# Two blocks of the A/B projection accumulated in the opening of layer 0, and one modulation group moved from layer 0's gate/up to layer 1's

## The chip, the cores and the metric

The kernel runs as one program on one core of a Trainium2 chip. The metric is the device time of one execution in microseconds (us). A core has a matrix engine (TensorE, PE), a vector engine (VectorE, DVE), a scalar engine (ScalarE, ACT), a general engine (GpSimd, POOL), a queue engine (SyncE, SP) that here only starts transfers, and sixteen DMA engines. Each engine works off its own list of instructions in order and waits on semaphores of the others. PE writes its products to PSUM, from where other engines fetch them.

## The reference, cut to what matters

The program computes two layers of an encoder on a sequence of 1024 tokens of width 1024:

```python
mod = silu(c) @ w_mod[l] + b_mod[l]                    # 1024 -> 6 * 1024
sh_a, sc_a, gt_a, sh_f, sc_f, gt_f = split(mod, 6)     # six modulation groups
h = rms_norm(x, g_attn[l]) * (1 + sc_a) + sh_a
proj = h @ w_in[l]                                     # columns of heads A, B and C
ya = neighborhood_attention(...); yb = sliding_window_attention(...); yc = axial_attention(...)
x = x + gt_a * (concat(rms_norm(ya), rms_norm(yb), rms_norm(yc)) @ w_o[l])
h = rms_norm(x, g_ffn[l]) * (1 + sc_f) + sh_f
gate, up = split(h @ w_gu[l], 2)                       # 2 * 2816 columns
x = x + gt_f * ((silu(gate) * up) @ w_down[l])
```

and a last `rms_norm` behind the second layer. All is in 32-bit floating point.

## The kernel before

**Products.** Each 32-bit operand is split into a high and a low part (`hh`/`hl` for the normalised activations, `whi`/`wlo` for weights), and a product is three matmuls (`mm3`: high x high, high x low, low x high) that accumulate in one PSUM tile of 128x512. A split is two passes: ACT writes the high part (a cast or copy), DVE, or POOL at some places, subtracts it and writes the low one. The activations are kept transposed: `hh[:, k, c]` is block `k` of eight (128 of the 1024 features) for the tokens `c`. A half is 512 tokens (`H`); layer 0 builds `hh`/`hl` for half 0 in the opening, pair of blocks by pair, and those for half 1 at the end of the opening (`h_blocks`).

**The opening of layer 0** needs the first two modulation groups before it has any block of `h`. For each pair `p` of blocks, 0 to 3, two loads `gm` of `w_mod` are multiplied by the condition (`gemv_half`: DVE adds, then a few PE matmuls into `ps_mod`), turned (`gemv_turn`, `ps_m`), and finished into shift and scale, after which `h_blocks(0, ...)` makes the two blocks (`pair_done`). Beside that, `c_first(n)` accumulates the C columns of half 0, block by block, into the four tiles `pssC` that stay open from pair 0 to the C section: 12 matmuls per block. Their weights come by `wc_stage` (SP starts the load into one of a small set of stage buffers `wst`) and `w_split`. `x_turn(1, ...)` transposes the second half of `x` into eight PSUM tiles `ps_x`, which ACT copies to `xt`; `spread` and `turn_vecs` (`pst`) follow, then `c_norm_first` and the four `h_blocks(1, ...)`. The pool `psl` of the opening has eight PSUM tiles with one tag; a new tile waits until the readers of the tile before it in its place are done.

**The C section and V projection** (about 76 to 175 us). Step `t` projects 128 tokens of C (`c_proj`), normalises and rotates the tiles of the step before, and transposes those of the step before that. Beside them run the A/B blocks `oc` 0 and 1 (`NE = 2`), and their results are taken out of PSUM by `ab_split`, which ACT and DVE do, and stored to a table in memory (`qkd`). The list `abs_` holds blocks that are projected and not yet split. V follows.

**The A/B section** (about 175 to 247 us) goes over `oc` = 2 to 7 and the two halves: `ab_proj` (24 matmuls into `ps_ab`), the store of the block before, the load of the weights two blocks on, at some steps `mod_sum` (four `ps_mod` matmuls), `z_step` (parts of a bias table), a number of `mod_one` (one 512 KB load of `w_mod` and DVE passes), and `ab_split`. Attention, the output projection, gate/up and down follow.

**Gate/up** takes 22 quads of columns, each with seven products (Strassen's scheme, so that sums of blocks are multiplied). `mod_stream` is a generator of the modulation groups that are left: each `next` does one step of a group, a 256 KB load `wmt` and a DVE pass into `acc`, and at the end of a group two flushes (`mod_parts` writes `acch` and `accl` on DVE, `mod_flush` makes two matmuls into `ps_mod` and two DVE passes). One step is taken behind each product from quad 7 on.

**Order.** Within the stages that are pinned (`pin(..., True)`) each engine issues in the order in which the code is written; so the list of calls in the opening and the tuples of `mod_one` counts set the order of the work.

The profile gives line 49 for every instruction, since a helper issues them all; so names of tiles, not lines, tell them apart.

Of the kernel before, what the change touches and what calls it, by code (L numbers as in the profile page):

```python
# [19 lines left out]
P = 128  # L20
D = 1024
S = 1024
# [63 lines left out]
def trunk(ctx: ExitStack, tc, A, C, out):  # L86
# [583 lines left out]
    def wc_stage(kp):  # L670
        st = stage()
        for dst, v in w_in_src(0, C_COLS, kp)(parts(st, 2)):
            sp.dma_start(dst, v)
        wcs.append(st)

    def c_first(n):

        wh, wl = wC[n // 2]
        for t in range(T0):
# [3 lines left out]
                n == 0, n == KC - 1,  # L683
            )

    def spill(half, ns=range(KC)):
        c = slice(half * H, (half + 1) * H)
        for n in ns:
            sp.dma_start(xd[:, n, c], xt[:, n, c])
# [8 lines left out]

    NE = 2
    T0 = 4  # L700
    wC, wcs = [], []
    pin((pe, act, dve, sp), True)
    c8 = stp.tile([KC, P], F32, name="c8")
# [5 lines left out]
    gm_load(0)  # L709
    gm_load(1)  # L710
    wc_stage(0)
    gm_load(2)
    rxs = [stp2.tile([P, 4], F32, name="rx", tag="rx", bufs=2) for _ in range(2)]
    act.activation(c8, c8, AF.Silu)
# [28 lines left out]

    gemv_half(0)
    gm_load(3)
    wc_stage(1)
    keep_busy(4)
    gemv_half(1)
    gm_load(4)
    xns[1].append(x_load(1, 0))  # L750
    w_split()
    wc_stage(2)
    keep_busy(2)
    pair_done(0)
    pssC = [psl.tile([P, 512], F32, name="ps_c", tag="mm") for _ in range(T0)]
    gemv_half(2)
    gm_load(5)
    xns[1].append(x_load(1, 1))
    c_first(0)
    w_split()  # L760
    wc_stage(3)
    c_first(1)
    gemv_half(3)
    gm_load(6)
# [1 line left out]
    gemv_half(4)  # L766
    gm_load(7)
    xns[1].append(x_load(1, 3))
    pair_done(1)
    x_square(1, 0, xns[1][0], rxs[1])  # L770
    c_first(2)
    c_first(3)
    w_split()
# [5 lines left out]
    gemv_half(6)  # L779
    pair_done(2)  # L780
    x_square(1, 1, xns[1][1], rxs[1])
    c_first(4)
    c_first(5)
    w_split()
# [4 lines left out]
    for j in (2, 3):  # L789
        x_square(1, j, xns[1][j], rxs[1])  # L790
    x_rms(rxs[1])
    x_turn(1, xns[1], range(4), (act, act))
    c_first(6)
    x_turn(1, xns[1], range(4, KC), (act, act))
# [1 line left out]
    spill(1)  # L796
    rows = spread(rxs[1], 0, psl)
    turn_vecs(1, v1)
    gm = stp.tile([P, 2048], F32, name="gm", tag="gm", bufs=3)
    first_t1 = c_norm_first(pssC[0], gm[:, 0:512], gm[:, 512:1024], gm[:, 1024:1032])  # L800

# [17 lines left out]
    for l in range(2):  # L819
# [158 lines left out]
        psc, psv = dict(enumerate(pssC)), {}  # L978
        qts, qns = {0: first_t1}, {}
        w = split_tile(wab.pop(0), KC, (ct, "wx", 2), dve)  # L980
        abs_ = []
        wV, vst = [], []

        def v_stage(kp):
# [193 lines left out]
        for oc in range(NE, 8):  # L1178
            w = wab
            for half in range(2):  # L1180
                if half == 0 and oc < 7:
                    sc = -0.125 if oc < 3 else None
                    wab = split_tile(wst.pop(0), KC, eng=dve, scale=sc)
                if oc == 6 and half == 0:
                    close(ps_cm)
                    psS_cm, psS = open_pool("psS", bufs=2, space=PSUM)
                    ps_cm, psl = open_pool("ps2", bufs=4, space=PSUM)
                scored = early_scores() if oc == 7 else None
                ps = ab_proj(w, half)
                if store:  # L1190
                    store(act)
                if scored:
                    scored()
                if half == 0 and oc < 6:
                    wst.append(w_ab(l, oc + 2))
                i = 2 * (oc - NE) + half
                if i % 4 == 2:
                    mod_sum()
                z_step()
                for _ in range((2, 2, 2, 1, 2, 1, 2, 1, 2, 1, 0, 0)[i]):  # L1200
                    mod_one()
                store = ab_split(oc, half, ps, ab)
        store(act)
        pin((pe, act, dve, pool), False)
        close(ab_cm)
# [816 lines left out]
            shifted_sub(b21, b21, shift(2 * i + 1), t2)  # L2022
            h_split("t4", i, b21, dve)

        mods_due = mod_stream(psl, (ntp, "sq", 2, H), (1, 3))
        bs = []
        rows = None
        norm = rstd_rows(ssq, ntp, psl)
# [24 lines left out]
        for q in range(NF):  # L2053
# [9 lines left out]
            for i, p in enumerate(PRODUCTS[2 if q < EARLY else 0 :]):  # L2063
# [2 lines left out]
                    act.activation(e, quads[q]["11"], AF.Silu)  # L2066
                ahead.fill()
                g_step()
                if q >= EARLY:
                    next(mods_due, None)  # L2070
        for _ in mods_due:
            pass
# [329 lines left out]
```

## Time and profile before

| what | us |
|---|---|
| median of three runs | 2403.49 |
| lowest and highest | 2403.01, 2408.04 |
| the profiled execution | 2405.66 |
| its span on the core | 2403.9 |
| opening, to the first `c_proj` of half 1 | 76.0 |
| A/B section, end of the last `ps_ab` | about 247 |
| gate/up of layer 0 (576.8 to 1013.7) | 436.9 |
| gate/up of layer 1 (1749.7 to 2173.6) | 423.9 |

Of the span PE is busy 97%, DVE 73%, ACT 50% and POOL 31%; the mean granted clock of PE is 0.993 of full. A row of the timeline gives start and length in us, engine, operation, the tile written and the tiles read; the time in brackets is how long the engine stood before it, and behind the arrow is what ended the wait. Rows with a count (x4) are several instructions that follow on each other. Matmuls overlap, so the distance of their starts, not the length of one, is what a matmul costs.

### The profile page before, as it was taken

How to read it: one execution, taken by the hardware profiler on the slowest of the kernel's cores; microseconds unless marked ns; L12 is line 12 of the kernel's file. 1: busy time of each engine (PE TensorE's matmuls, PEld its weight loads, DVE VectorE, ACT ScalarE, POOL GpSimd, SP SyncE). 2: the span in 40 equal slices, each digit the busy share in tenths (PEclk: the TensorE clock that was granted, in tenths of full speed). 3: DMA queues.
4: the chain of work that ended last, by engine and by line, in shares of the span. 5: the costliest groups of instructions: out<-in, count | busy, mean ns of one | idle time of the engine just before them, and what ended most of it. 6: DMA issues, size and time to landing. Idle time of an engine off the chain costs nothing. (4 is left out here: it accounts for less than half of the span.)

```text
span 2403.9 us, 33342 instructions
## 1 busy us (share of the span) xinstructions
PE 2337.2 (97%) x11733; PEld 1954.9 (81%) x11733; DVE 1756.9 (73%) x2788; ACT 1192.2 (50%) x2250; POOL 744.0 (31%) x719
## 2 busy tenths in 40 slices
PE   8999999999999999999999999999999999999998
PEld 4788899888787887888887879988888888888886
DVE  5767898977858788587677679988797554547765
ACT  3422788944543333344543148897454334334443
POOL 1431345610244443300036114465004443430001
PEclk9999999999999999999999999999999999999999
DMA  8458316154345454586424761152534333329633
GB/s 265 138 183 278 94 62 156 45 201 129 109 137 171 155 186 152 174 265 197 155 88 123 246 215 28 44 145 74 199 103 145 114 101 106 122 88 298 213 125 110
DMA packets 305336, 356.95 MB, mean 148 GB/s; under 512 B 51964, under 2 KB 221788, under 8 KB 305168
## 3 DMA queue, kind: packets, MB, share of 16 engines
q1 hardware_dynamic: 283296, 342.07, 44.9%
q10 hardware_dynamic: 21504, 12.59, 2.0%
q8 instruction: 92, 1.51, 0.3%
q14 instruction: 76, 0.62, 0.1%
q0 software_dynamic: 368, 0.17, 0.0%
HBM read 269.79 MB, written 88.63 MB: 149 GB/s over the span
## 5 line engine op out<-in xcount | busy, mean ns | idle before, releaser
L49 PE MATMUL ps_d<-wpt 128*128 128x512 f32 x1848 | 423.8, 390 | 1.1 <-ACT wpt L49 0.7
L49 PEld LDWEIGHTS ps_d<-wpt 128*128 128x128 f32 x1848 | 345.7, 188 | 74.4 <-issue 3.0
L49 POOL TENSOR_SCALAR pr<-pr,rs 128x1024 f32<-128x1024 f32 (+2 forms) x248 | 193.0, 791 | 220.8 <-DVE rs L49 196.8
L49 POOL TENSOR_TENSOR sg<-sg,u 128x512 f32<-128x512 f32 x82 | 116.6, 1422 | 354.0 <-ACT sg L49 228.4
L49 PE MATMUL pv<-pt,vs 128*128 128x256 f32 x1088 | 175.8, 296 | 17.7 <-DVE y L49 13.4
L49 DVE TENSOR_TENSOR pt<-T,pt 128x512 fp32r<-128x512 f32 x272 | 176.9, 678 | 8.3 <-ACT pt L49 8.0
L49 ACT CAST wpt<-w 128x512 fp32r<-128x512 f32 x154 | 95.7, 621 | 174.6 <-PE ps_d L49 156.1
L49 ACT CAST pt<-T 128x512 fp32r<-128x512 f32 x272 | 151.8, 584 | 40.6 <-PE T L49 38.8
L49 ACT COPY u<-ps_w 128x512 f32<-128x512 f32 x128 | 75.1, 587 | 190.1 <-PE ps_w L49 190.1
L49 POOL TENSOR_TENSOR wpt<-ws,wpt 128x512 fp32r<-128x512 f32 x80 | 110.9, 1388 | 186.5 <-ACT wpt L49 140.3
L49 DVE TENSOR_TENSOR wpt<-w,wpt 128x512 fp32r<-128x512 f32 x154 | 108.9, 707 | 79.8 <-ACT wpt L49 77.7
L49 PEld LDWEIGHTS pv<-pt,vs 128*128 128x128 f32 x1088 | 141.7, 190 | 30.8 <-DVE y L49 26.0
L49 PE MATMUL T<-identr,pr 128*128 128x128 f32 x1176 | 161.6, 273 | 0.8 <-DVE edge L49 0.4
L49 PEld LDWEIGHTS T<-identr,pr 128*128 128x128 f32 x1176 | 137.9, 140 | 16.0 <-issue 1.3
L49 DVE SCALAR_TENSOR_TENSOR acc<-wmt,condT,acc 128x512 f32<-128x512 f32 (+1 forms) x98 | 113.9, 1172 | 44.6 <-DMA wmt<-in_w_mod_dram 44.2
L49 ACT CAST wpt<-ws 128x512 fp32r<-128x512 f32 x176 | 107.8, 622 | 60.0 <-issue 28.1
L49 DVE TENSOR_TENSOR wpt<-ws,wpt 128x512 fp32r<-128x512 f32 x96 | 82.9, 872 | 62.0 <-ACT wpt L49 61.9
L49 DVE TENSOR_TENSOR wpt<-graw,wpt 128x512 fp32r<-128x512 f32 x154 | 110.1, 715 | 17.4 <-ACT wpt L49 17.4
L49 ACT CAST wpt<-graw 128x512 fp32r<-128x512 f32 x154 | 95.0, 617 | 52.9 <-DMA graw<-gpd 48.8
L49 DVE TENSOR_REDUCE rs<-sC 128x1 f32<-128x1024 f32 x88 | 107.3, 1221 | 17.7 <-PE sC L49 12.3
L49 DVE TENSOR_TENSOR ws<-wr 128x512 f32<-128x512 f32 x88 | 78.9, 899 | 53.9 <-POOL wpt L49 50.8
L49 PE MATMUL sC<-qk 128*128 128x512 f32 x384 | 107.5, 403 | 5.8 <-ACT pr L49 5.6
(300 smaller groups left out, 5938.0 us busy)
## 6 DMA issues: line engine op xcount, KB each, us to landing
wr<-in_w_gu_dram SPq DMA_DIRECT2D x92, 512.0 KB, 4.1
gpd<-sg SPq DMA_DIRECT2D x154, 256.0 KB, 4.4
graw<-gpd SPq DMA_DIRECT2D x76, 512.0 KB, 3.5
w<-in_w_down_dram SPq DMA_DIRECT2D x110, 256.0 KB, 5.6
wmt<-in_w_mod_dram SPq DMA_DIRECT2D x48, 512.0 KB, 5.3
qk<-qkd SPq DMA_DIRECT2D x44, 512.0 KB, 7.1
wst<-in_w_o_dram SPq DMA_DIRECT2D x32, 512.0 KB, 4.1
wmt<-in_w_mod_dram SPq DMA_DIRECT2D x64, 256.0 KB, 3.6
```

Of the source, the lines that this page charges most:

```text
L49: ins = op(*args, **kwargs)
```

## The change

The four parts of the change are these.

1. *Opening.* `a_stage(u)` loads the weights of A/B block 2 + u, and `a_split(u)` splits them (one ACT and one DVE pass of 128x1024, with the factor -0.125) into blocks of `hh`/`hl` of the second half, 6 and 7 for u = 0, 4 and 5 for u = 1, which are not needed until `h_blocks(1, ...)`. `a_first(u, p)` does the six matmuls of half 0 for the pair `p` of blocks into `pssA[u]`. The last three `wc_stage` come one step later.
2. *C section.* `abs_` begins with these two finished blocks, so their `ab_split` stands ahead of the normalisation of C step 0 and their eight stores are started by SP.
3. *A/B section.* `oc` 2 and 3 leave out half 0; the counts of `mod_one` sum to 16 as before, in another order, and the first `mod_sum` comes one step later in layer 0.
4. *Gate/up.* The stream of layer 0 ends with group (1, 1) and not with (1, 2), so three groups are left there and not four; the A/B section of layer 1 takes (1, 2), (1, 3), (1, 4), and one group is left for layer 1's gate/up, (1, 5). No step is taken behind products 2 and 5 of a quad.

```diff
+    def a_stage(u):
+        ast.append(w_ab(0, EARLY_AB[u]))
+    def a_split(u):
+        st = parts(ast.pop(0), 2)
+        hi, lo = (t[:, 6 - 2 * u : 8 - 2 * u, H:S] for t in (hh, hl))
+        act.activation(hi, st, AF.Copy, scale=-0.125)
+        dve.scalar_tensor_tensor(
+            out=lo, in0=st, scalar=-0.125, in1=f32(hi), op0=ALU.mult, op1=ALU.subtract
+        )
+    def a_first(u, p):
+        for k in (2 * p, 2 * p + 1):
+            n, c = 6 - 2 * u + k // 4, slice(H + k % 4 * P, H + k % 4 * P + P)
+            mm3(
+                pssA[u], hh[:, n, c], hl[:, n, c], hh[:, k, 0:H], hl[:, k, 0:H],
+                k == 0, k == KC - 1,
+            )
...
+    EARLY_AB = (2, 3)
...
     wc_stage(0)
+    a_stage(0)
     gm_load(2)
...
     gemv_half(0)
     gm_load(3)
-    wc_stage(1)
     keep_busy(4)
     gemv_half(1)
     gm_load(4)
     xns[1].append(x_load(1, 0))
+    a_split(0)
     w_split()
-    wc_stage(2)
+    wc_stage(1)
     keep_busy(2)
     pair_done(0)
     pssC = [psl.tile([P, 512], F32, name="ps_c", tag="mm") for _ in range(T0)]
+    pssA = [psl.tile([P, 512], F32, name="ps_ab", tag="mm") for _ in range(2)]
     gemv_half(2)
     gm_load(5)
+    a_stage(1)
     xns[1].append(x_load(1, 1))
     c_first(0)
     w_split()
-    wc_stage(3)
+    wc_stage(2)
     c_first(1)
...
     xns[1].append(x_load(1, 3))
+    wc_stage(3)
     pair_done(1)
+    a_split(1)
     x_square(1, 0, xns[1][0], rxs[1])
+    a_first(0, 0)
     c_first(2)
     c_first(3)
...
     x_square(1, 1, xns[1][1], rxs[1])
+    a_first(1, 0)
+    a_first(0, 1)
     c_first(4)
     c_first(5)
...
     x_rms(rxs[1])
+    a_first(1, 1)
     x_turn(1, xns[1], range(4), (act, act))
     c_first(6)
     x_turn(1, xns[1], range(4, KC), (act, act))
...
     turn_vecs(1, v1)
+    for u in (1, 0):
+        for p in (2, 3):
+            a_first(u, p)
...
-        abs_ = []
+        abs_ = [] if l else [(oc, 0, ps) for oc, ps in zip(EARLY_AB, pssA)]
...
-                ps = ab_proj(w, half)
+                early = l == 0 and half == 0 and oc in EARLY_AB
+                ps = None if early else ab_proj(w, half)
...
-                if i % 4 == 2:
+                if i in ((2, 6, 10) if l else (3, 6, 10)):
                     mod_sum()
                 z_step()
-                for _ in range((2, 2, 2, 1, 2, 1, 2, 1, 2, 1, 0, 0)[i]):
+                for _ in range(
+                    (2, 2, 2, 1, 2, 1, 2, 1, 2, 1, 0, 0)[i]
+                    if l else (0, 2, 0, 3, 2, 2, 2, 2, 2, 1, 0, 0)[i]
+                ):
                     mod_one()
-                store = ab_split(oc, half, ps, ab)
+                store = None if early else ab_split(oc, half, ps, ab)
...
-        mods_due = mod_stream(psl, (ntp, "sq", 2, H), (1, 3))
+        mods_due = mod_stream(psl, (ntp, "sq", 2, H), (1 + l, 2 - 2 * l))
...
-                if q >= EARLY:
+                if q >= EARLY and i % 3 != 2:
                     next(mods_due, None)
```

The first place is on PE in the opening, the first four tiles of `x_turn(1, ...)` and the start of `c_first(6)` (`ps_x` is written by transposes of `xn`, the loaded rows of `x`; a wait on Activation is one for ACT, and that on DMA for a load). Before:

```order
L49 MATMUL ps_x<-identr,xn 128x128 [waits DMAHW4_49]
L49 MATMUL ps_x<-identr,xn 128x128 [waits PE_49]
L49 MATMUL ps_x<-identr,xn 128x128 x7
L49 MATMUL ps_x<-identr,xn 128x128 [waits DVE_49]
L49 MATMUL ps_x<-identr,xn 128x128 x3
L49 MATMUL ps_c<-whi,hh 128x512 [waits Activation_49]
L49 MATMUL ps_c<-whi,hl 128x512 [waits DVE_49]
```

In the changed kernel:

```order
L49 MATMUL ps_x<-identr,xn 128x128 [waits DMAHW5_49]
L49 MATMUL ps_x<-identr,xn 128x128 [waits DVE_49]
L49 MATMUL ps_x<-identr,xn 128x128 x3
L49 MATMUL ps_x<-identr,xn 128x128 [waits Activation_49]
L49 MATMUL ps_x<-identr,xn 128x128 x3
L49 MATMUL ps_x<-identr,xn 128x128 [waits Activation_49]
L49 MATMUL ps_x<-identr,xn 128x128 x3
L49 MATMUL ps_c<-whi,hh 128x512
L49 MATMUL ps_c<-whi,hl 128x512 [waits DVE_49]
```

The third and the fourth tile, which waited for nothing of ACT, now each wait for it.

The second place is on DVE at the beginning of the C section, between the last blocks of `h` (`hl<-nt,...`) and the normalisation of C step 0 (`TENSOR_REDUCE r<-csq`; the numbers behind names count tiles). Before:

```order
L49 SCALAR_TENSOR_TENSOR hl<-nt,mod_82,hh 128x512 [waits Activation_49] x2
L49 CAST t5h<-t_428 32x6 [waits DMAHW4_49]
L49 TENSOR_TENSOR t5h<-t_428,t5h 32x6 [waits DVE_49]
L49 TENSOR_TENSOR wlo<-wst,whi 128x1024 [waits DMAHW5_49,DMAHW1_49,Activation_49]
L49 TENSOR_REDUCE r_738<-csq 128x8 [waits Activation_49]
```

In the changed kernel:

```order
L49 SCALAR_TENSOR_TENSOR hl<-nt,mod_82,hh 128x512 [waits Activation_49] x2
L49 CAST t5h<-t_444 32x6 [waits DMAHW6_49]
L49 TENSOR_TENSOR t5h<-t_444,t5h 32x6 [waits DVE_49]
L49 TENSOR_TENSOR wlo<-wst,whi 128x1024 [waits DMAHW5_49,DMAHW7_49,DMAHW2_49,Activation_49]
L49 TENSOR_TENSOR qko<-ps_ab,qko 128x8x8x8 [waits PE_49,Activation_49]
L49 TENSOR_TENSOR qko<-ps_ab,qko 128x8x8x8 [waits DMASW2_49,DMASW1_49,DMASW3_49,DMASW0_49,Activation_49]
L49 TENSOR_REDUCE r_810<-csq 128x8 [waits DMASW1_49,DMASW2_49,Activation_49,Pool_49]
```

Two low halves of A/B blocks (`qko`) stand ahead of the normalisation.

The third place is on DVE in layer 0's gate/up, from the first flush's `accl` of the second group there to the second flush's (`ws` and `wpt` are sums and low parts of weights, `u` and `sg` the results taken from PSUM). Before:

```order
L49 TENSOR_TENSOR accl<-acc,acch 128x512
L49 TENSOR_TENSOR ws<-ws,wr 128x512
L49 TENSOR_TENSOR wpt<-ws,wpt 128x512
L49 TENSOR_TENSOR sg<-sg 128x512
L49 TENSOR_TENSOR ws<-wr 128x512
L49 TENSOR_TENSOR ws<-wr,ws 128x512
L49 TENSOR_TENSOR sg<-sg,ps_w 128x512
L49 TENSOR_TENSOR wpt<-wr,wpt 128x512
L49 CAST acch<-acc 128x512
L49 TENSOR_TENSOR acc<-ps_mod,identr 128x512
L49 TENSOR_TENSOR accl<-acc,acch 128x512
```

In the changed kernel:

```order
L49 TENSOR_TENSOR accl<-acc,acch 128x512
L49 TENSOR_TENSOR ws<-ws,wr 128x512
L49 TENSOR_TENSOR wpt<-ws,wpt 128x512
L49 TENSOR_TENSOR sg<-sg 128x512
L49 TENSOR_TENSOR ws<-wr 128x512
L49 TENSOR_TENSOR ws<-wr,ws 128x512
L49 TENSOR_TENSOR sg<-sg,ps_w 128x512
L49 TENSOR_TENSOR wpt<-wr,wpt 128x512 x2
L49 TENSOR_TENSOR u<-u,ps_w 128x512
L49 TENSOR_TENSOR acc<-ps_mod,identr 128x512
L49 CAST acch<-acc 128x512
L49 TENSOR_REDUCE sums<-acc 128x4
L49 TENSOR_TENSOR accl<-acc,acch 128x512
```

One `wpt` and one `u` now stand between the two flushes in addition; they belong to the product that was added there.

More of the change, by code (lines that the diff above doesn't have):

```diff
@@ L700, in trunk @@
     T0 = 4
+    EARLY_AB = (2, 3)
+    ast = []
     wC, wcs = [], []
```

## The prediction

> **What bounds the kernel now.** I read the page's first lines, then the windows by stage, then the tensor engine's waits and timeline in the stages that the change touches.
>
> ```profile
> span 2403.9 us, 33342 instructions
> ...
> PE 2337.2 (97%) x11733; PEld 1954.9 (81%) x11733; DVE 1756.9 (73%) x2788; ACT 1192.2 (50%) x2250; POOL 744.0 (31%) x719
> ```
>
> PE is busy for 97% of the span, so the kernel is as long as PE's work plus its holes. The change removes no matmul; it can win only by filling holes and by letting matmuls run at full clock. The windows (length, then busy time and count of PE, PEld, DVE, ACT, POOL, granted clock, DMA share, GB/s) say where holes are:
>
> ```profile
> 20.00:30.00 10.00, 10.00 (x28) 5.57 (x27) 7.16 (x11) 3.84 (x5) 0.00 (x0) 0.66 1.00 336
> 50.00:60.00 10.00, 9.11 (x28) 5.63 (x27) 4.45 (x6) 2.77 (x5) 2.76 (x3) 0.83 0.18 46
> 70.00:80.00 10.00, 5.21 (x18) 3.64 (x17) 7.61 (x12) 2.77 (x6) 4.72 (x4) 0.75 0.91 337
> 80.00:90.00 10.00, 10.00 (x42) 8.17 (x41) 9.29 (x16) 5.33 (x9) 0.00 (x0) 0.91 0.28 97
> 190.00:210.00 20.00, 20.00 (x90) 16.54 (x89) 14.69 (x17) 2.73 (x4) 0.00 (x0) 1.00 1.09 328
> 210.00:230.00 20.00, 20.00 (x90) 16.54 (x89) 13.96 (x16) 4.27 (x6) 0.00 (x0) 1.00 0.75 257
> 576.80:1013.70 436.90, 428.81 (x1878) 351.83 (x1877) 331.43 (x425) 176.00 (x308) 168.50 (x117) 1.00 0.46 150
> 1749.70:2173.60 423.90, 421.87 (x1862) 347.97 (x1861) 247.04 (x324) 176.89 (x308) 159.32 (x117) 1.00 0.35 114
> ```
>
> The opening (to about 90 us) has holes and a reduced clock; the A/B section (about 175 to 247) has no hole; gate/up of layer 0 takes 436.9 us against 423.9 us for the same products in layer 1, an excess of 13.0 us. The holes of the opening, from PE's timeline (start, length, instruction, and in brackets the idle time ahead and what ended it):
>
> ```profile
> 38.38 0.50 PE L49 MATMUL ps_c<-whi,hh 128*128 128x512 f32 x1 [1.99 <-ACT hh L49]
> ...
> 49.67 0.50 PE L49 MATMUL ps_c<-whi,hh 128*128 128x512 f32 x1 [1.99 <-ACT hh L49]
> ...
> 51.82 0.63 PE L49 MATMUL ps_c<-wlo,hh 128*128 128x512 f32 x1
> 52.24 0.63 PE L49 MATMUL ps_c<-whi,hh 128*128 128x512 f32 x1
> ...
> 60.11 0.40 PE L49 MATMUL ps_m<-identr,gr 1*128 1x1 f32 x4 [0.72 <-ACT gr L49]
> 60.45 1.97 PE L49 MATMUL ps_x<-identr,xn 128*128 128x128 f32 x16
> 62.51 0.50 PE L49 MATMUL ps_c<-whi,hh 128*128 128x512 f32 x1
> 63.29 0.50 PE L49 MATMUL ps_c<-whi,hl 128*128 128x512 f32 x1 [0.28 <-DVE hl L49]
> ...
> 66.20 2.12 PE L49 MATMUL ps_x<-identr,xn 128*128 128x128 f32 x16
> ...
> 71.37 0.23 PE L49 MATMUL pst<-identr,v 72*128 72x72 f32 x1
> 76.01 0.80 PE L49 MATMUL ps_c<-whi,hh 128*128 128x512 f32 x1 [4.41 <-ACT hh L49]
> ```
>
> Three holes wait for a new pair of `hh` blocks. After the second, matmuls start 0.42 us apart (51.82 to 52.24). In the A/B section they start 0.227 us apart, 20 steps in 4.54 us between these two rows:
>
> ```profile
> 241.97 0.39 PE L49 MATMUL ps_ab<-hh,whi 128*128 128x512 f32 x1
> ...
> 246.51 0.39 PE L49 MATMUL ps_ab<-hl,whi 128*128 128x512 f32 x1
> ```
>
> **The change, part by part.**
>
> *The 48 matmuls that move.* In the A/B section they cost 48 x 0.227 = 10.9 us, all on the path (PE is busy 20.00 of 20 us). In the opening, 6 go into the hole of 38.38 (1.4 of 1.99 us), 12 into that of 49.67 (2.7 us, 0.7 too many), 6 ahead of 60.45, and 24 (5.5 us, 1.0 too many) into that of 76.01. Filling the second hole probably spares the slow stretch behind it: eight matmuls at 0.42 instead of 0.23 were 1.5 us. So `ps_m` of pair 3 comes about 1.4 us earlier than 60.11 and, behind six matmuls of 1.4 us, `ps_x` at 60.4 as before.
>
> *Two more loads and splits in the opening.* A load of 512 KB at 336 GB/s is 1.6 us of a DMA that is full in the window from 20 to 30, and has room (share 0.18) from 50 on. A split is one ACT and one DVE pass of 128x1024 (a row of each engine's timeline):
>
> ```profile
> 63.02 1.04 ACT L49 ACTIVATE xt<-xn 128x1024 f32<-128x1024 f32 x1
> ...
> 87.08 1.23 DVE L49 TENSOR_TENSOR wlo<-wst,whi 128x1024 fp32r<-128x1024 f32 x1
> ```
>
> These engines stand 3 to 7 us of each 10 in these windows. I cost loads and splits at nothing, covered by those gaps; if the cover is gone, a pair comes up to 1.6 + 1.2 = 2.8 us late.
>
> *The PSUM tiles.* The opening's pool has eight. `pssC` holds four, now `pssA` two, so two are left for the transposes of `x`, which before found four: 60.45 ran without a wait. In the changed order the third and the fourth wait for ACT, with `c_first(6)` queued behind them on PE. What ACT does there (its timeline):
>
> ```profile
> 61.73 1.39 ACT L49 ACTIVATE hh<-nt,mod 128x512 fp32r<-128x512 f32 x2 [1.67 <-DVE nt L49]
> ...
> 65.58 3.98 ACT L49 COPY xt<-ps_x 128x512 f32<-128x512 f32 x8
> ```
>
> The copies that free tiles (3.98/8 = 0.5 us each) stand behind `hh` and two squares: 65.58 - 1.4 = 64.2. PE does two tiles (1.0 us, to 61.4), stands for 3.3 us until 64.7, does the other two, and begins `c_first(6)` at 65.7 instead of 62.5, 3.2 us late. Waits that stood behind it before (0.28 us for `hl`, some in the 2.12 us of 66.20) are then over; I give back 0.9. So `pst` ends 2.3 us later. If the new hole brings the half clock, the twelve matmuls of `c_first(6)` cost 12 x 0.2 = 2.4 us more; at half weight that makes 3.5 us (0 to 4.7).
>
> [...]
>
> *The end of the opening.* The 24 matmuls run while DVE builds the second half's blocks (its timeline):
>
> ```profile
> 74.45 1.40 DVE L49 SCALAR_TENSOR_TENSOR nt<-xt,gsc,ps_r 128x512 f32<-128x512 f32 x2
> ...
> 88.22 0.68 DVE L49 TENSOR_REDUCE r<-csq 128x8 f32<-128x512 f32 x1
> ```
>
> This chain, not PE, sets when the C section can go on, so the filled hole of 4.41 us shifts nothing by itself. Between 87.08 and 88.22 DVE now also does the low halves of two finished blocks, ahead of the normalisation:
>
> ```profile
> L49 DVE TENSOR_TENSOR qko<-ps_ab,qko x8: 672/679/691, 100.7 to 200.9; 128x512 fp32r<-128x512 f32 x8
> ```
>
> Two of 0.68 us, overlapped a little, are 1.2 us of delay. POOL's `wlo` hangs on the same chain, and PE waited for it already:
>
> ```profile
> 116.94 0.50 PE L49 MATMUL ps_ab<-hh,wlo 128*128 128x512 f32 x1 [0.31 <-POOL wlo L49]
> ```
>
> So the V projection begins 3.5 + 1.2 = 4.7 us later (1.2 if the tiles cost nothing, 5.9 with the half clock in full).
>
> *The A/B section.* It loses 10.9 us of matmuls. The weights of two blocks are wanted one half (24 x 0.227 = 5.4 us) sooner; for that I take 0.6 us of waiting for a split. What attention's first steps wait for is partly a store (a DVE row and a PE row):
>
> ```profile
> 255.05 2.36 DVE L49 TENSOR_REDUCE rs<-sC 128x1 f32<-128x1024 f32 x2 [2.57 <-DMA qkd<-qko]
> 257.57 1.20 PE L49 MATMUL sC<-qk 128*128 128x512 f32 x4 [3.36 <-ACT pr L49]
> ```
>
> That `qkd` store belongs to the last block and moves up with it, unless the DMA, at 1.09 and 0.75 (0.92) over the 40 us of the two rows above, is the limit. I take 9.1 of the 10.3 us (5 to 10.3; no loss, since each queue there gets less work). Opening and A/B section together: 4.7 - 9.1 = -4.4 us.
>
> *The modulation group.* Its sixteen loads, its DVE passes and its four `ps_mod` matmuls pass from one gate/up to the other, so the matmuls sum to nothing. Of layer 0's 13.0 us excess, 16 x 0.227 = 3.6 are matmuls and 6.1 are holes (436.90 - 428.81 = 8.1, less 423.90 - 421.87 = 2.0); the remaining 3.3 are matmuls that ran slower. PE's waits in layer 0's gate/up (us in total, times, longest):
>
> ```profile
> PE ps_w L49 <- ACT u L49: 3.1, 3, 1.4
> PE ps_mod L49 <- DVE accl L49: 2.2, 2, 1.5
> PE ps_mod L49 <- DVE acch L49: 1.6, 2, 1.2
> ```
>
> Layer 0 keeps three of four groups, skips two products of seven, and has up to three products instead of two between the two flushes of a group: `acch` and `accl` get more time, and DVE (331 of 437 us) less work. Layer 1's DVE has 247 of 424 us and one group to bear. The bounds: layer 0 keeps its stalls and layer 1 pays an average group, 13.0/4 - 0.9 = 2.3 us lost; or all stalls go, 9.4 us won. I take 6.5, nearer the upper end, since 3.8 of the 6.1 us of holes are at the flushes, which now stand further apart, and slow matmuls follow holes.
>
> **Sum.** -4.4 - 6.5 = -10.9 us against the profiled execution of 2405.66 us (1.8 us more than its span). That execution is 2.2 us above the median of 2403.49 us, so in the median: 2392.6 us.
>
> **The rivals.**
>
> 1. *Attention starts on the DMA's time.* For it: the share of 1.09 and the 2.57 us wait for `qkd`. Against it: 0.75 in the next 20 us. The section wins 5 instead of 9.1: 2396.7.
> 2. *The gate/up gain does not come*, as stalls move with the group. For it: the largest wait, for `u`, is at no flush. Against it: layer 1's DVE load. The sum is -4.4: 2399.1, just inside the 0.2% (4.8 us) that a measurement of this kernel can tell from no change.
> 3. *The tiles cost nothing*: ACT comes to its copies early and no slow stretch follows. Against it: ACT's queue above. V starts 1.2 us late, the section wins 10.3, gate/up 9.4: -18.5, 2385.0.
> 4. *Slower: the half clock stays*, from the new hole at 61.4 into the C section. For it: the window from 70 to 80 has 0.75 behind the hole of 4.41 us. Against it: 0.91 in the next, though PE still waited there. A matmul at 0.42 loses 0.19 of 0.227, so each us of matmul work loses 0.85. It decides where 10.9 + 4.8 = 15.7 us are lost, with 18.5 us of work slow, from 65.7 to about 100 us; held until 116.94, with 51 us of slow time or 28 of work, it gives +23.5: 2416.
>
> **How the numbers follow.** Chances: forecast 0.48; rival 1 0.19; rival 2 0.15; rival 3 0.12; rival 4 0.06. Half of rival 2, and a little of rival 1 where gate/up wins less, lie inside 0.2% (0.11); rival 4, and 0.02 of rival 2 where layer 1 loses, are slower (0.08); the rest, 0.81, is faster. The range goes from 1 us below rival 3 to where rivals 1 and 2 meet (4.7 - 5 = -0.3, less a small gain of 1 in gate/up: 2402.2): 2384 to 2402. It leaves out rival 4 and some 0.1 at both ends.
>
> **What would show it.** Right: a hole of about 3 us inside the `ps_x` tiles ended by ACT; none over 1 us ahead of the last `ps_c` of the opening; the first `ps_ab` of the A/B section 4 to 6 us late, and the first `sC` 4 to 5 us early; both gate/ups near 427 us. Wrong: a granted clock under 0.9 for more than 15 us between 60 and 120; holes in the A/B section ended by DMA; layer 0's gate/up above 433 us or layer 1's above 430.

## The result, and the profile after

The changed kernel takes 2399.41 us (median of 20 runs, 2396.08 to 2404.63) against 2403.25 us of the one before (20 runs, 2398.92 to 2412.84). The medians are 3.8 us apart. The ratio of the times is 0.9981 with a 95% interval of 0.9975 to 0.9988, which is 4.6 us faster (2.9 to 6.0), just inside the 0.2% that the prediction counts as no change, where 10.9 us were forecast. The two profiled executions differ by more, 2395.5 against 2403.9 us of span. An execution of either kernel scatters over 8 us and more, so one pair of profiles says where time went, and not by how much the kernels differ.

The windows of the changed kernel, same columns as before (the A/B section now begins at 181.6):

```profile
20.00:30.00 10.00, 7.93 (x31) 4.65 (x30) 7.32 (x11) 3.86 (x5) 0.00 (x0) 1.00 1.03 343
50.00:60.00 10.00, 9.28 (x40) 6.12 (x39) 5.55 (x8) 3.95 (x6) 1.08 (x2) 1.00 0.36 97
60.00:70.00 10.00, 6.79 (x33) 5.62 (x32) 3.35 (x7) 6.00 (x11) 1.98 (x2) 0.83 0.91 330
70.00:80.00 10.00, 9.76 (x54) 8.02 (x53) 2.62 (x6) 3.05 (x6) 0.12 (x1) 1.00 0.55 206
80.00:90.00 10.00, 9.83 (x42) 7.05 (x41) 9.60 (x14) 4.21 (x6) 4.64 (x4) 1.00 0.15 49
181.60:196.00 14.40, 13.13 (x58) 10.55 (x57) 11.91 (x14) 4.61 (x6) 4.60 (x3) 1.00 0.60 189
196.00:216.00 20.00, 20.00 (x90) 16.54 (x89) 18.74 (x24) 2.14 (x3) 0.00 (x0) 1.00 1.04 335
216.00:236.00 20.00, 20.00 (x89) 16.53 (x89) 15.58 (x16) 4.97 (x7) 0.00 (x0) 1.00 0.93 318
242.00:262.00 20.00, 15.48 (x77) 13.24 (x76) 11.23 (x15) 10.44 (x19) 4.43 (x4) 0.83 0.84 246
577.20:1004.40 427.20, 425.09 (x1874) 350.11 (x1873) 313.26 (x400) 176.19 (x308) 167.77 (x117) 1.00 0.44 143
1737.90:2163.80 425.90, 423.28 (x1866) 348.66 (x1865) 266.20 (x350) 176.05 (x309) 161.94 (x117) 1.00 0.38 124
```

The hole between 70 and 80 is filled (5.21 before, 9.76 now) and a new one has come between 60 and 70 (9.44 us busy before, 6.79 now). Layer 0's gate/up lost 9.7 us (436.9 to 427.2), layer 1's took 2.0 more. PE's timeline in the opening:

```profile
35.38 1.02 PE L49 MATMUL ps_mod<-ga,onesr 128*1 128x512 f32 x2 [1.72 <-DVE ga L49]
...
39.59 0.50 PE L49 MATMUL ps_c<-whi,hh 128*128 128x512 f32 x1 [0.41 <-ACT hh L49]
...
59.80 0.40 PE L49 MATMUL ps_m<-identr,gr 1*128 1x1 f32 x4 [0.72 <-ACT gr L49]
...
61.63 1.04 PE L49 MATMUL ps_x<-identr,xn 128*128 128x128 f32 x8
65.89 1.66 PE L49 MATMUL ps_x<-identr,xn 128*128 128x128 f32 x8 [3.21 <-ACT xt L49]
...
68.20 0.63 PE L49 MATMUL ps_c<-wlo,hh 128*128 128x512 f32 x1
68.62 0.63 PE L49 MATMUL ps_c<-whi,hh 128*128 128x512 f32 x1
...
76.62 0.23 PE L49 MATMUL pst<-identr,v 72*128 72x72 f32 x1
```

Two tiles of `x` are transposed, then PE stands for 3.21 us until ACT has copied the first, and in this execution the matmuls behind it run at half pace (0.42 us apart, 68.20 to 68.62). A wait that was not there before stands at 35.38: the second pair's modulation is late. Further on PE waits for split weights behind the C section and in the A/B section (`wlo`), and in attention's first steps (`pv`, `sC`):

```profile
123.59 0.50 PE L49 MATMUL ps_ab<-hh,wlo 128*128 128x512 f32 x1 [1.42 <-POOL wlo L49]
...
188.65 0.50 PE L49 MATMUL ps_ab<-hh,wlo 128*128 128x512 f32 x1 [1.27 <-DVE wlo L49]
...
250.31 0.39 PE L49 MATMUL pv<-pt,vs 128*128 128x256 f32 x1 [2.41 <-ACT pt L49]
...
256.27 1.20 PE L49 MATMUL sC<-qk 128*128 128x512 f32 x4 [2.10 <-ACT pr L49]
```

Before, these last two began at 251.70 and 257.57. PE reaches attention 2.2 us earlier (244.5 for 246.7), but its second step is only 1.3 us ahead, the clock in the window from 242 to 262 is 0.83 where it was 1.00, and attention ends at 475.9, behind the 475.7 of before. The window of the kernel before:

```profile
242.00:262.00 20.00, 14.92 (x88) 12.55 (x87) 12.10 (x18) 10.29 (x19) 3.98 (x4) 1.00 0.87 259
```

PE's waits in gate/up, layer 0 and then layer 1:

```profile
PE ps_w L49 <- ACT u L49: 1.4, 2, 0.7
PE ps_w L49 <- ACT wpt L49: 0.6, 1, 0.6
PE ps_w L49 <- ACT sg L49: 0.2, 1, 0.2
```

```profile
PE ps_w L49 <- ACT u L49: 1.4, 3, 0.8
PE ps_w L49 <- ACT wpt L49: 0.6, 1, 0.6
PE ps_w L49 <- ACT sg L49: 0.6, 1, 0.6
```

No wait of `ps_mod` is left in either layer.

### The profile page after: what moved, and what is told of

It reads as the page before. It is cut to its first block, busy times and chain, and to the rows that moved or that the text cites. A ratio compares the mean times of both kernels' runs of the same rounds, so it can differ in the third digit from the quotient of the medians.

```text
span 2395.5 us, 33339 instructions
## 1 busy us (share of the span) xinstructions
PE 2332.5 (97%) x11733; PEld 1952.1 (81%) x11733; DVE 1759.4 (73%) x2790; ACT 1192.5 (50%) x2252; POOL 747.9 (31%) x719
## 5 line engine op out<-in xcount | busy, mean ns | idle before, releaser
L49 POOL TENSOR_TENSOR sg<-sg,u 128x512 f32<-128x512 f32 x82 | 118.0, 1440 | 352.0 <-ACT sg L49 227.6
L49 DVE TENSOR_TENSOR wpt<-w,wpt 128x512 fp32r<-128x512 f32 x154 | 108.8, 707 | 80.3 <-ACT wpt L49 78.1
```

Source lines behind the costliest of these rows:

```text
L49: ins = op(*args, **kwargs)
```

## The experiments

The changes below are against the changed kernel unless it is said otherwise. The table gives, from the timeline of each profile, when `pst`, the V projection and attention begin (first `ps_v`, first `sC` or `T` behind the last projection), the end of attention's last matmul ahead of the output projection, and how long gate/up of each layer took; and the ratio of the times to the kernel before, where it was timed. Kernels without a ratio ran once, for the profile.

| kernel | pst | V | attention | its end | gate/up 0 | gate/up 1 | ratio (95%) |
|---|---|---|---|---|---|---|---|
| before | 71.4 | 129.5 | 246.7 | 475.7 | 436.9 | 423.9 | 1 |
| before_again | 69.1 | 127.2 | 244.4 | 473.3 | 436.1 | 424.1 | |
| gateup_only | 70.8 | 129.4 | 246.6 | 477.8 | 432.6 | 426.2 | 0.9979 (0.9968 to 0.9990) |
| changed | 76.6 | 136.1 | 244.5 | 475.9 | 427.2 | 425.9 | 0.9981 (0.9975 to 0.9988) |
| after_again | 74.7 | 134.2 | 243.9 | 474.6 | 427.8 | 426.2 | |
| opening_only | 75.9 | 135.4 | 243.8 | 475.6 | 437.0 | 423.3 | 0.9994 (0.9985 to 1.0003) |
| turn_two | 72.6 | 132.9 | 241.1 | 474.1 | 427.8 | 425.1 | 0.9962 (0.9948 to 0.9975) |
| turn_two_again | 72.2 | 132.6 | 240.6 | 473.6 | 426.9 | 425.9 | 0.9970 (0.9958 to 0.9983) |
| rows_late | 76.8 | 136.2 | 248.7 | 475.7 | 430.1 | 425.6 | 0.9985 (0.9976 to 0.9993) |
| turn_rows | 72.3 | 131.4 | 242.2 | 471.3 | 432.8 | 426.4 | 0.9965 (0.9952 to 0.9977) |
| rows_early | 77.5 | 137.0 | 254.3 | 482.4 | 430.4 | 425.7 | 1.0010 (1.0001 to 1.0019) |
| turn_early | 73.6 | 132.7 | 250.9 | 479.2 | 430.1 | 426.8 | 0.9989 (0.9978 to 1.0000) |
| turn_early_splits | 74.1 | 133.7 | 250.6 | 481.5 | 429.9 | 425.5 | 0.9996 (0.9987 to 1.0005) |
| one_block | 75.7 | 134.6 | 248.5 | 478.4 | 429.2 | 426.2 | 0.9996 (0.9984 to 1.0007) |
| stage_later | 81.5 | 141.0 | 250.6 | 482.0 | 428.0 | 426.9 | |
| no_skA | 74.6 | 134.1 | 247.6 | 477.7 | 429.0 | 425.8 | |
| turn_no_skA | 73.6 | 132.7 | 245.6 | 473.6 | 429.7 | 426.3 | |

### Both kernels a second time

> The kernel before, unchanged, profiled a second time. Theory A (the hole of 2.6 us at the second group's flushes and the slow matmuls behind it belong to the kernel): gate/up of layer 0 takes 435 to 438 us again. Rival B (they are an accident of one execution): it takes under 432 us, and the span comes out 4 us or more below 2403.9.

> The changed kernel, unchanged, profiled a second time. Theory A: gate/up of layer 0 takes 427 us again, attention begins 2 us earlier than before (about 244.5) and ends where it ended before (about 476). Rival B (the first profile was a lucky execution): layer 0's gate/up takes over 430 us, or the span is above 2398.

Theory A holds for gate/up: 436.1 and 427.8 us. In the changed kernel attention began at 243.9 and ended at 474.6, somewhat ahead of the 244.5 and 476 of theory A. For the kernel before, the span was 2398.6, 5.3 us under the first, as rival B had it for the span: what differed was the opening, 2.3 us shorter, and the stretch between the two gate/ups, 2.2 us shorter. In this execution the clock between 20 and 30 us was 1.00, where it was 0.66 in the first; so the slow clock of the opening belongs to the execution and not to the kernel.

### The two halves of the change

`gateup_only` is the kernel before with the moved group:

```diff
-        mods_due = mod_stream(psl, (ntp, "sq", 2, H), (1, 3))
+        mods_due = mod_stream(psl, (ntp, "sq", 2, H), (1 + l, 2 - 2 * l))
...
-                if q >= EARLY:
+                if q >= EARLY and i % 3 != 2:
```

> The moved modulation group and its pace alone, the opening as before. Theory A (all of the gain is here, and the rest of the change gives about nothing): 4 to 8 us faster than the kernel before, layer 0's gate/up at 427 us and layer 1's at 426, about as much as the whole change. Rival B (the gain is the opening's, gate/up differs from execution to execution only): within 2 us of the kernel before.

`opening_only` is the changed kernel with these two edits undone.

> The blocks accumulated in the opening, with the A/B section as changed, and gate/up with its four groups as before. Theory A: the opening loses 6.6 us up to the V projection, the A/B section wins 8.8, attention's first steps give the 2.2 back: within 1.5 us of the kernel before. Rival B: 3 us or more faster.

The group alone is 5.0 us faster than before (2.4 to 7.7), as much as the whole change; the opening and the A/B section alone 1.5 us (0.7 slower to 3.6 faster), no difference that these runs can tell from none. In the first the waits for `ps_mod` are gone, in the second they are all there (PE's waits in layer 0's gate/up, `gateup_only` and then `opening_only`):

```profile
PE ps_w L49 <- ACT u L49: 2.2, 2, 1.4
PE ps_w L49 <- ACT sg L49: 1.3, 2, 1.1
PE ps_st L49 <- DVE ssq L49: 1.2, 1, 1.2
```

```profile
PE ps_w L49 <- ACT u L49: 3.1, 3, 1.4
PE ps_mod L49 <- DVE accl L49: 2.2, 2, 1.5
PE ps_mod L49 <- DVE acch L49: 1.5, 2, 1.2
```

Layer 0's gate/up took 432.6 us in `gateup_only`, not the 427 of theory A, with waits at other places; the profile caught the longest of its twelve executions (2407.30 us, 8 above their median). Over all fourteen profiles with the edit it took 427 to 433 us, 429.4 in the mean, and layer 1's 426.0; the three without it took 436.7 and 423.8 in the mean. So layer 0 gains 7.3 us, layer 1 loses 2.3, and the 5.0 us that are left are what the times of `gateup_only` give.

### The hole inside the transposes of x

`turn_two` gives PE the two tiles that have a place, then the six matmuls and `c_first(6)`, then the other six tiles:

```diff
-    a_first(1, 1)
-    x_turn(1, xns[1], range(4), (act, act))
-    c_first(6)
-    x_turn(1, xns[1], range(4, KC), (act, act))
+    x_turn(1, xns[1], range(2), (act, act))
+    a_first(1, 1)
+    c_first(6)
+    x_turn(1, xns[1], range(2, KC), (act, act))
```

> The changed kernel with two transposed tiles of x ahead of the six matmuls of the last early pair and of c_first(6), and the other six behind them: so PE has work while ACT is not yet at its copies. Theory A (the hole of 3.2 us inside the ps_x tiles is the main loss of the opening): the hole is gone, pst ends 3 to 5 us earlier than 76.6 and the V projection begins at 130 to 133 instead of 134 to 136. If attention's start hangs on PE, 3 to 4 us faster than the changed kernel; rival B (attention's first steps hang on transfers): V comes earlier, but the end of attention moves by less than 1.5 us.

> The kernel with the tiles of x in two and six once more, unchanged. Theory A (the gain over the changed kernel is real): 6 to 11 us faster than the kernel before, V at 131 to 133, attention's end at 471 to 474.5. Rival B (the first five runs were lucky): 3 to 6 us faster, as the changed kernel.

The hole is gone (PE's timeline, `turn_two`):

```profile
59.97 1.09 PE L49 MATMUL ps_x<-identr,xn 128*128 128x128 f32 x8
...
65.73 1.14 PE L49 MATMUL ps_x<-identr,xn 128*128 128x128 f32 x8
67.06 1.15 PE L49 MATMUL ps_x<-identr,xn 128*128 128x128 f32 x8 [0.19 <-ACT xt L49]
...
72.56 0.23 PE L49 MATMUL pst<-identr,v 72*128 72x72 f32 x1
...
250.10 0.58 PE L49 MATMUL pv<-pt,vs 128*128 128x256 f32 x1 [5.62 <-ACT pt L49]
255.94 1.19 PE L49 MATMUL sC<-qk 128*128 128x512 f32 x4 [1.85 <-ACT pr L49]
```

`pst` comes 4.1 us earlier than 76.62 and V 3.2 earlier; in the repeat it is nearly the same. Of these, less than half arrives at attention's end in the profiles: PE reaches attention 3.4 us earlier (241.1 for 244.5), and the hole ahead of `pv` is 5.62 us long where it was 2.41. This hole differs between executions of one kernel (1.88 us in `after_again`, 4.61 in `opening_only`, 4.41 in `turn_two_again`); in the means of three and of two profiles PE comes 3.2 us earlier, the hole is 2.0 us longer, and the end comes 1.5 us earlier (473.9 for 475.4). So the hole inside the transposes was the opening's main loss (theory A), while at attention the end moves by no more than the 1.5 us that rival B allowed, and by less than half of what PE gained. Against the kernel before, the times are 0.9962 and 0.9970: 7 to 9 us faster (medians 2395.35 and 2395.59 us). Both medians are some 4 us below the changed kernel's, and the ratios differ from its 0.9981 by 4.6 and 2.6 us; the first interval touches the changed kernel's at 0.9975, the second overlaps it, so that the gain over the changed kernel rests on both together. It is more than the 1.5 us at attention's end; where the rest comes from is not shown.

### One block for two

`one_block` sets `EARLY_AB = (2,)` and leaves out the load, split, tile and matmuls of the second.

> The changed kernel with one early block (oc 2) instead of two: one load, one split, 24 matmuls, one PSUM tile. Theory A (the loss of the opening comes with the second tile and the second set of loads and splits more than with the first): V begins at 129.5 to 132, less than half of the 6.6 us late; the A/B section wins 5.4 us less its wait. Rival B (each block costs the same): V at 131.5 to 133. In both cases the A/B section gains about half, and the kernel is within 2 us of the changed one.

`pst` and V come as late as with two blocks, 75.7 and 134.6, and neither theory foresaw the reason: three free tiles don't help. PE takes the third tile and stands at the fourth for 4.46 us, since ACT's first copy comes no earlier (timeline of `one_block`):

```profile
60.19 1.53 PE L49 MATMUL ps_x<-identr,xn 128*128 128x128 f32 x12
...
66.18 1.11 PE L49 MATMUL ps_x<-identr,xn 128*128 128x128 f32 x4 [4.46 <-ACT xt L49]
```

The first block pays nearly all of the opening's loss, and only half of the A/B section's gain is left (343.8 us from V to attention's end, where two blocks have 340.1 and none 346.9): 0.9996.

### The early load, and the place of the splits

`stage_later` moves `a_stage(0)` from ahead of `gm_load(2)` to behind `gm_load(3)`.

> The changed kernel with the first early load of weights behind the fourth load of w_mod instead of ahead of the third. Theory A (this 512 KB load makes the second pair's modulation late): the wait of ps_mod for ga at 35 us falls from 0.7 to 1.7 us to under 0.4, and c_first(2) begins about 1.6 us earlier than 39.2 to 39.6. Rival B (the two splits on DVE make it late): it stays within 0.5 us.

The wait of `ps_mod` for `ga` is gone, but only since PE itself is late, so the run can't choose between the two. The split `a_split(0)` stands ahead of `w_split` and of the first pair on ACT and DVE, and both engines now wait for its later load: `c_first(0)` has a hole of 4.52 us at 30.05, and all is 5 us later.

The profiles of the two kernels answer the question. First the kernel before (SP starts the second load of C weights, ACT makes its high part without a wait), then the changed kernel:

```profile
18.32 0.51 SPq L49 DMA_DIRECT2D wst<-in_w_in_dram  x1
...
26.18 1.03 ACT L49 CAST whi<-wst 128x1024 fp32r<-128x1024 f32 x1
```

```profile
23.45 0.37 SPq L49 DMA_DIRECT2D wst<-in_w_in_dram  x1
...
30.78 1.05 ACT L49 CAST whi<-wst 128x1024 fp32r<-128x1024 f32 x1 [3.76 <-DMA wst<-in_w_in_dram]
...
31.87 1.23 DVE L49 TENSOR_TENSOR wlo<-wst,whi 128x1024 fp32r<-128x1024 f32 x1 [2.08 <-ACT whi L49]
```

There are two stage buffers `wst`, and the early block takes the second one. So the second load of C weights has to wait until a buffer has been read: the early split's pass on DVE ends at 23.43, and the load starts at 23.45 instead of 18.32. ACT waits 3.76 us for it, DVE 2.08 us for ACT, and the second pair's `ga` passes stand behind that `wlo` on DVE. The early split itself is 1.14 us of DVE ahead of them. Together that is about the 3.3 us by which DVE takes longer from its first split to the last `ga` pass (11.8 us before, 15.1 now; in `after_again` 14.1, with 1.11 us of waiting). Both theories have a part of it, then, and theory A's load does its part by the buffer that it holds. In `one_block` the same wait is 3.76 us: the first block alone brings it.

`turn_early_splits` splits the two blocks behind the first part of the normalisation and not ahead of it (on top of `turn_early`, below).

> That, and the two early splits behind the normalisation of C step 0 instead of ahead of it. Theory A (they stand in the chain of DVE with their full 1.2 us): V begins 0.8 to 1.3 us earlier than without this edit. Rival B (DVE is the bound of the C section anyway, and the splits cost the same wherever they stand): V within 0.4 us.

From `pst` to V it is 59.6 us, against 59.1 in `turn_early`, and V begins 1.1 us later: no gain, so theory A is out, though the 0.4 us of rival B are exceeded. The change itself has 59.5 there and the kernel before 58.1. On DVE the two low halves of finished blocks (`qko`) make the way from `wlo` to the normalisation's `r` 1.2 us longer (92.56 to 94.91, before 87.08 to 88.22), and this move didn't win them back.

### What attention's first steps wait for

The rows of the kernel before showed `rs` waiting for a `qkd` store. In all these kernels ACT itself starts the last two of these stores, and its copies `pt`, for which PE's `pv` waits, stand behind that start in its order. In the changed kernel the start takes 2.21 us, in `turn_two` 5.42, and the trace puts the end of the wait to the landing of `skA<-skr`, the 1 MB table of layer 1 (ACT in `turn_two`):

```profile
243.51 5.42 ACTq L49 DMA_DIRECT2D qkd<-qko  x2
248.97 1.57 ACT L49 CAST pt<-T 128x512 fp32r<-128x512 f32 x3 [6.22 <-DMA skA<-skr]
```

In all seventeen profiles the first `pt` begins 0.04 to 0.05 us behind the end of this start, and attention ends 223.8 to 227.6 us behind it; behind PE's own arrival at attention it is 227.0 to 233.1 us. So an earlier PE finds ACT held up by the start of a transfer, and attention's end goes by that. Three ways were tried to take `skA`, and the six `skB` (1.5 MB) beside it, out of that place.

> The changed kernel with the ten transfers that fill skA of layer 1 and skB (2.5 MB) started at step 8 of attention's pipeline instead of step 4, behind the loads of vs and ahead of their first reader at about 306 us. Theory A (the last qkd stores and the first pieces of attention wait in the DMA engines behind these transfers): the wait for qkd at about 255 us is gone, the holes of PE between 245 and 262 fall from 4.5 us to under 2, and attention's end comes 2 to 4 us earlier. Rival B (they wait for each other for another reason): the holes stay, within 1 us of the changed kernel.

This edit did something else than its expectation says: SP's order isn't fixed from step 6 on, and the transfers (they are seven, one `skA` and six `skB`; the expectation's ten is a slip) were issued between 128 and 211 us, not later. Attention ended as before (475.7): ACT now waited 3.1 us for loads of `vs`, which moved up into the place.

> Both of the two edits, tiles of x in two and six, and skA/skB later. If both theories A hold they add: attention ends 5 to 8 us earlier than in the changed kernel, at 467 to 471 us, and the kernel is 8 to 12 us faster than the one before. If only one holds, 2 to 4 us faster than the changed kernel.

Here the edits of `turn_two` and `rows_late` together gave an end of 471.3, 2 to 3 us below `turn_two`, but the kernel isn't faster than `turn_two` (0.9965). So theory A is not borne out by `rows_late` and not excluded by `turn_rows`.

`rows_early` has the transfers at a fixed place, at the beginning of the A/B section.

> The changed kernel with the ten transfers into skA of layer 1 and skB (2.5 MB) put into SP's fixed order at the beginning of the A/B section (about 150 us) instead of at the start of attention. Theory A (at attention's start the qkd stores wait in the DMA engines and on their semaphores behind these transfers, so that PE's earlier arrival is given back): the wait for qkd goes, the matmul of sC behind the second hole begins at 252 to 254 instead of 255.1 to 257.5, attention ends at 470 to 473 instead of 474.6 to 475.9. Rival B (attention's start hangs on the stores for themselves, or on the loads of vs behind them): it stays at 255 or later.

> That, and the tiles of x in two and six. Theory A: V begins at 131 to 133, sC behind the second hole at 249 to 252, attention ends at 467 to 470.5, and the kernel is 8 to 12 us faster than the one before. Rival B: V begins as early, but attention ends at 473 or later, as with the tiles of x alone.

In `rows_early` attention ends 6.5 us later than in the changed kernel, and in `turn_early`, which adds the edit of `turn_two`, 5.1 later than in `turn_two`, for a new reason: PE waits for the split of the A/B section's first weights, where it waits for nothing in the changed kernel (the 1.27 us there stand at the next block). That split stands on DVE behind passes that wait for loads of `w_mod` (`wmt`; timeline of `rows_early`, PE and then DVE, and DVE's split in the changed kernel):

```profile
189.17 0.80 PE L49 MATMUL ps_ab<-hh,wlo 128*128 128x512 f32 x1 [6.31 <-DVE wlo L49]
```

```profile
168.97 0.85 DVE L49 TENSOR_SCALAR acc<-wmt,condT 128x1024 f32<-128x1024 f32 x1 [17.16 <-DMA wmt<-in_w_mod_dram]
...
186.90 2.21 DVE L49 SCALAR_TENSOR_TENSOR wlo<-wst,whi 128x1024 fp32r<-128x1024 f32 x1
```

```profile
174.46 1.23 DVE L49 SCALAR_TENSOR_TENSOR wlo<-wst,whi 128x1024 fp32r<-128x1024 f32 x1 [1.05 <-ACT whi L49]
```

The weights themselves were there: ACT makes their high part at 174.28, for 173.37 in the changed kernel. But SP starts the moved transfers from 147 to 157 us, and its first load of `w_mod` behind them at 163.47, where the changed kernel has 147.66.

`no_skA` and `turn_no_skA` leave the 1 MB transfer out altogether.

> The changed kernel without the 1 MB transfer into skA of layer 1 at attention's start; layer 1 then reads its bias table from skA of layer 0, so that this part of the result isn't computed. Theory A (qkd's last store waits for this transfer): it is issued some 2 to 5 us earlier than 248.6, sC behind the second hole begins at 250 to 254 instead of 255.1 to 257.5. Rival B (the stores are slow for their own number, or wait for vAd and vs): 255 to 257.5 again.

> The same, with the tiles of x in two and six, so that PE comes 3 us earlier. Theory A: the hole of 5.6 us ahead of the first pv (250.1 with the tiles alone) falls under 3 us, sC behind the second hole begins at 248 to 252, and attention ends at 466 to 471. Rival B: the hole stays over 4.5 us and attention ends at 473 or later.

The end doesn't come earlier: 477.7 against 474.6 to 475.9, and with the tiles 473.6, as in `turn_two`. The hole ahead of `pv` falls from 5.62 to 1.97 us in the second, but PE reaches attention 4.5 us later than in `turn_two`, since ACT, which takes the last block out of PSUM, now waits for another transfer (waits of `turn_no_skA` and of `turn_two`, all engines, 238 to 262 us):

```profile
ACT qko L49 <- DMA vs<-vAd: 4.1, 1, 4.1
...
PE pv L49 <- ACT pt L49: 2.0, 1, 2.0
```

```profile
ACT pt L49 <- DMA skA<-skr: 6.2, 1, 6.2
...
PE pv L49 <- ACT pt L49: 5.6, 1, 5.6
```

Without `skA` the loads of `vs` come up into its place and ACT waits for them. The start of the last stores did get free: in the seven kernels that have `skA` elsewhere or not at all it takes 1.24 to 1.27 us. But where the loads of `vs` moved up (`rows_late`, `turn_rows`, `no_skA`, `turn_no_skA`) ACT waited for them one step earlier, 3.1 to 5.1 us, so that the start itself came later. So it isn't this transfer alone; attention's first steps hang on ACT in a stretch in which `vAd`, `skA`, `skB` and `vs` are all under way. Which limit it is, the transfers' own time or the order in which ACT's queue may start them, stays open; `turn_rows`, with the earliest end, shows that some time can be won there.

## Why the prediction was wrong

The direction was right; the gain was 4.6 us where 10.9 were forecast. The time, 2399.41 us, is almost that of rival 2 (2399.1), but by the opposite way: rival 2 had the gain in the opening and the A/B section and none in gate/up, and the runs have it the other way round. Of the signs that were named, the hole of 3 us ended by ACT and the two gate/ups near 427 us came; the first `ps_ab` of the A/B section was 6.5 us late in the first pair of profiles (4 to 6 forecast), and the first `sC` 2.8 us early (4 to 5). By the prediction's own terms, with means over the profiles of kernels that share the stage (opening and A/B section: before, `before_again`, `gateup_only` against changed, `after_again`, `opening_only`; gate/up: before, `before_again`, `opening_only` against changed, `after_again`, `gateup_only`):

| term | forecast | measured |
|---|---|---|
| `ps_m` of pair 1, the second of 0 to 3 (loads and splits "at nothing") | 0 | +2.4 (34.5 to 36.9) |
| from there to `ps_m` of pair 3 (the filled holes) | -1.4 | -2.0 (24.7 to 22.6) |
| `pst` | +3.5 | +5.3 (70.4 to 75.7) |
| from `pst` to V (the two splits) | +1.2 | +1.2 (58.3 to 59.5) |
| V projection begins | +4.7 | +6.5 (128.7 to 135.2) |
| from V to attention's end (the A/B section) | -9.1 | -6.8 (346.9 to 340.1) |
| opening and A/B section together | -4.4 | -0.2; timed alone -1.5 (-3.6 to +0.7) |
| gate/up, both layers | -6.5 | -5.1 in the profiles (-7.5 and +2.3); timed alone -5.0 (-7.7 to -2.4) |

**The step that failed** is the sum of the opening and the A/B section: "4.7 - 9.1 = -4.4 us". Both of its halves were off in the same direction by some 2 us, and little was left. The remaining 1.4 us are missing in gate/up.

*The opening.* The mechanism of the PSUM tiles was right, in place and in size: a hole of 3.21 us was found where 3.3 were worked out, from `ps_m` of pair 3 to `pst` it is 16.2 us in the mean where 11.2 were before (5.0 more, 4.9 forecast), and `turn_two`, which takes the hole away, gains 4.1 us at `pst` against the first profile and 3.2 against the mean. The filled second hole brought what was worked out, too: from `ps_m` of pair 2 to that of pair 3 it is 12.8 us in the three old profiles and 11.3 in the new ones. What failed is "I cost loads and splits at nothing, covered by those gaps". The second pair comes 2.4 us later, for 2.8 that the forecast named as the price without cover, and so the gain of the filled holes is gone again. The early block's load holds one of the two stage buffers, the next load of C weights starts 5 us later, and DVE, which works off its passes in order, waits for it ahead of the second pair's (2.08 us, for ACT's high part of these weights, for whose load ACT waits 3.76 us). The gaps were read from the engines' busy time; what counts is whether an engine is free at the moment when the pair hangs on it.

*The A/B section.* Up to attention it went nearly as forecast: from V to attention's start 117.2 us became 108.8, 8.4 less, with 1.27 us of waiting for a split in the first profile where 0.6 was assumed. Then attention's first steps took back 1.6 us in the mean and 2.4 in the first pair of profiles. The forecast had the row, the 2.57 us wait of `rs` for `qkd`, and counted that it "moves up with" the last block; rival 1 had it the other way, with 5 us. The truth lay between, at 6.8. The store did not move up with the block: PE reached attention 1.8 us earlier in the mean (245.9 to 244.1), but ACT was done with starting the last stores only 0.4 us earlier (249.6 to 249.3), and its copies for attention stand behind that. These 1.5 us are nearly all of the 1.6. PE's arrival alone doesn't set the end: `turn_two` brought PE 3.2 us earlier in the mean, and attention's end 1.5.

*The modulation group.* The mechanism held. All of the waits for `acch` and `accl` are gone from layer 0, and layer 1 pays 2.0 to 2.3 us, about the 2.3 that the forecast's lower bound has for an average group. The size came out 1.4 to 1.5 us short: layer 0 gains 7.5 us in the mean of three profiles. By the first pair of profiles alone (9.7 less 2.0) the term would have looked too small and not too large; 427.2 us is near the lower end of the fourteen, 426.9 to 432.8.

*The rivals.* Rival 2 (no gain in gate/up) and rival 3 (the tiles cost nothing) did not occur. Rival 4, the half clock that stays, did not: it came behind the new hole in some executions (0.83 between 60 and 70 in the changed kernel, 1.00 in `after_again`) and was over after 3.4 us in the changed kernel (granted clock 0.50 from 66.25 to 69.67; another such stretch, 250.57 to 253.99, was as long). Where it came, `pst` is 16.8 and 16.6 us behind `ps_m` of pair 3, where it didn't, 15.3. So it costs some 1.4 us in two of three executions, and the 1.2 us that half a weight gave it were about right. What decides whether a hole brings it these runs don't show. PE was busy for 6.79 us between 60 and 70 in the changed kernel and for 6.78 in `after_again`. In the kernel before there were two holes of 1.99 us: behind the one that ended at 38.38 the clock was 1.00 up to the next hole (38.38 to 47.60), behind the one that ended at 49.67 it was 0.50 from 51.06 to 54.48.

## What to carry to other kernels

Work that is moved into holes can take more than the holes' time: its loads, its splits, its stage buffers and its PSUM tiles are taken from the engines and loads that made the holes. Here that made the second pair 2.4 us later, and PE stood 3.21 us for a tile. Ask of each buffer which load now has to wait for it. Before counting a gain at the end of a stage, see what the next stage's first step waits for: if it is a transfer, PE's earlier arrival can turn into a longer hole (in `turn_two` PE came 3.4 us earlier, and the hole ahead of `pv` grew from 2.41 to 5.62 us). And where a fixed set of tiles gets smaller, give PE in its order as many writers as there are tiles, and then other work, before the next one that needs a copy; that edit was worth some 3 to 4 us here, and the version with it is 7 to 9 us faster than the kernel before.

## What was not expected of the hardware

- The same program's opening differs by 2.3 us between executions whose clock between 20 and 30 us differs (0.66 and 1.00 in the two profiles of the kernel before), and behind a hole of 3.2 us at the same place the clock was 0.50 for 3.4 us in one execution of the changed kernel (66.25 to 69.67) and 1.00 in the next (60 to 70 in `after_again`).
- A transfer that is taken away need not shorten a wait for it: without the 1 MB `skA`, ACT waited 4.1 to 5.1 us for loads of `vs` that moved into its place, and attention's end was the same to 0.5 us in `turn_no_skA` and some 2 us later in `no_skA`.
- 2.5 MB of transfers ahead of the `w_mod` loads of the A/B section (`rows_early`) made DVE wait 17.16 us for the first of these loads, with the DMA engines not full (a share of 0.63 and 0.73 between 147 and 170 us) but the load started 16 us later, and a split of weights that needs none of them 12 us late (186.90 for 174.46); PE waited 6.31 us for it.
- ACT, which starts transfers beside its passes, stood while a start waited: it took 5.42 us for the start of two `qkd` stores in `turn_two`, and its next pass began 0.04 us behind it.
